# A hybrid attention layer on one core: first merge weights ahead of the attention outputs, and mixed blocks ahead of later gate weights on the load queue

## The chip, the cores and the metric

The kernel runs on one core of a Trainium2 chip. The metric is the device time of one execution in microseconds (us), as the median of several runs. A profile of one execution gives for each engine what ran when: PE is the matrix engine (PEld its weight loads), DVE the vector engine, ACT the scalar engine, POOL the third elementwise engine, and SP the engine that issues most of the loads and stores. Each engine works through its own list of instructions strictly in the listed order; an instruction whose data are not there holds up all that stand behind it on that engine.

## What is computed

One layer of an encoder, for 1024 tokens of width 1024, all in float32:

```python
proj = (rms_norm(x, g_norm1) * (1 + sc1) + sh1) @ w_in
qa, ka, va, qb, kb, vb, gates = split(proj)
o_a = neighbourhood_attention(qa, ka, va, rpb)            # 8 heads, 512 columns
o_b = dilated_window_attention_merged(qb, kb, vb)         # 3 groups of 4 heads, 256 columns after merging
gate_a, gate_b = split(sigmoid(gates + b_gate))
merged = gate_a * (o_a @ w_proj_a) + gate_b * (o_b @ w_proj_b)
x = x + gt1 * (merged @ w_o)
a, up = split((rms_norm(x, g_norm2) * (1 + sc2) + sh2) @ w_ffn_in)
x = x + gt2 * ((silu(a) * up) @ w_ffn_out)
```

The change lies in the part that computes `gates` (a product of the normalised input with 2048 columns of `w_in`) and then `merged`.

## The kernel before

Every float32 matrix operand is written as a sum of two parts of a narrower format that the matrix engine takes, called hi and lo. ACT copies the operand into hi (lines 124 and 1180), then DVE or POOL subtracts hi from the operand and writes lo (lines 125 and 1181). A product of two such operands is three matrix multiplications: hi by hi, hi by lo, lo by hi. The order of the matrix instructions on PE is the order of the program text. On the other engines a scheduler inside the compiler sets the order, from the program order and its own estimate of times, except that an instruction given to `pin` (`tc.keep_in_program_order`) keeps its place relative to the others that are pinned. The order is fixed when the kernel is built.

The gates are computed for eight blocks of 128 channels, each with a Strassen-like scheme of seven half-size products called w11, w12, x1, x4 and then x2, x3, w22. Here `prod` means 12 matrix multiplications of 128x128 by 128x512, for half of the depth. The four first products of each block run either inside the attention stage or, for blocks 3 and 4, right after it (`cover`). Then the three last products run in three groups (`gate_group`): blocks (3, 4, 5), then (6, 7, 2), then (0, 1); in each group x2 of all its blocks, then x3, then w22. So after the attention PE has 8 products of `cover`, 9 + 9 + 6 of the groups, 32 in all.

The right-hand operands of x2, x3 and w22 are sums and differences of blocks of the normalised input, the mixed blocks. They lie ready in device memory (`t_d`), and `mixed_load` brings one (two loads of 1 MB) into a part of the tile `hT` when its former content is no longer needed: x2 after w11, x3 after w12, and w22 after x4.

The weights of the last products come by `gate_late_load` (per block one load of 512 KB and one of 256 KB into a tile named `gl`), and `gate_late` makes of them x2, x3 and w22: two subtractions on DVE (lines 1124 and 1125), then hi and lo of each. lo of x2 and x3 is DVE's, lo of w22 is POOL's. `gate_late` of a block of the next group stands behind one of the three phases of a group. The results are added on DVE into accumulators named `sg` (line 1136), partly on POOL (line 1138), and go through a sigmoid on ACT (line 1092). `gate_acc` loads the partial sums of a block from the store `sig_d` into `sg`.

`w1_combos` prepares sums of weights for a much later stage: a load of 1 MB, four sums on DVE (lines 1115 to 1118) and four stores. `o_split` loads the attention outputs (six pieces, `o_d`, 512 KB each in two halves) into buffers named `raw` and splits them into the tiles `oT`; pieces 0 to 3 belong to the first attention, 4 and 5 to the second. `merge` computes a block of `merged` in two halves of 512 tokens: for each half 12 matrix multiplications of `oT` 0 to 3 (bank t or v), then 6 of `oT` 4 and 5 (bank d or s). Its weights come by `merge_w` (`wpa` and `wpb`, also through `raw`), with lo by POOL. There are six `raw` buffers, and six tiles that the gate weights, `w1_combos` and `oT` share in turn.

Of the kernel before, what the change touches and what calls it, by code (L numbers as in the profile page):

```python
# [25 lines left out]
EARLY = tuple(i for k in range(6) for i in (k, k + HT))  # L26
AHEAD, OTURN = 6, {1: 6, 5: 7}
MORD = (3, 4, 5, 6, 7, 2, 0, 1)
GPAIRS, GGROUPS = ((5, 6), (7, 2), (0, 1), (3, 4)), ((3, 4, 5), (6, 7, 2), (0, 1))
# [18 lines left out]
def hybrid_layer(ctx: ExitStack, tc: tile.TileContext, x, colp, wada1, wada2, bada2, wqkv, wg, wpa, wpb,  # L48
                 wo, w1, w2, hgain, ropeg, rope, rbias, bmask, g2r, out):
    nc = tc.nc  # L50
# [18 lines left out]
    t_d = tc.dram_tile([2, 4, 128, 4, 512], F32, name="t_d")  # L69
# [42 lines left out]
    def fview(ap):  # L112
        return ap.bitcast(F32)

    def wload(src, n):
        raw = wp.tile([128, 512], F32, tag="raw", bufs=NRAW, name="raw")
        nc.sync.dma_start(raw[:, :n], src)
        return raw[:, :n]

    def wsplit(r, eng=None):  # L120
        n = r.shape[1]
        hi = wp.tile([128, 512], F32R, tag="hi", bufs=NHL, name="whi")
        lo = wp.tile([128, 512], F32R, tag="lo", bufs=NHL, name="wlo")
        nc.scalar.activation(hi[:, :n], r, AF.Copy)  # L124
        (eng or nc.gpsimd).tensor_sub(lo[:, :n], r, fview(hi[:, :n]))  # L125
        return hi, lo

    def wslot(src, n):
        return wsplit(wload(src, n))
# [56 lines left out]
    def unit_load(u, k):  # L186
        return wload(wqkv[u, :, k, :], 384)
# [510 lines left out]
    def mm_set(pb, wsl, src, ksrc, n, ntot, done, hs):  # L698
        for j in range(n):
            for i, (a, b) in enumerate(PASS):  # L700
                nc.tensor.matmul(pb, wsl[a][:, j * 128:(j + 1) * 128], src[b][:, ksrc + j, hs],
                                 start=(done == 0 and j == 0 and i == 0),
                                 stop=(done + j == ntot - 1 and i == 2))

    gwt, gacc, gbank, graw = {}, {}, {}, {}

    def hblk(k, c):
        return [z[:, 4 * k:4 * k + 4, 512 * c:512 * c + 512] for z in hT]

    TBLK = {"w11": (0, 0), "w12": (1, 0), "x4": (1, 1), "x1": (0, 1), "x2": (0, 0), "x3": (1, 0), "w22": (1, 1)}  # L710
    TD = {"x1": 0, "w22": 1, "x3": 2, "x2": 3}

    def mixed_load(nm):
        for q in range(2):
            nc.sync.dma_start(fview(hblk(*TBLK[nm])[q]), t_d[q, TD[nm]])

    def gate_raw(i, q):
        return wload(wg[i, :, 4 * q:4 * q + 4, :], 512)

    def gate_land(z, i, q0, q1):  # L720
        nc.sync.dma_start(z[:, 512 * q0:512 * q1], wg[i, :, 4 * q0:4 * q1, :])
        for q in range(q0, q1):
            graw[i, q] = z[:, 512 * q:512 * q + 512]

# [5 lines left out]
    def gate_prep(p, part):  # L730
        pr = GPAIRS[p]
        if part == 0:
            for i in pr if p == 0 else ():
                for q in (0, 1):
                    graw[i, q] = gate_raw(i, q)
            for nm, q in (("w11", 0), ("w12", 1)):
                for i in pr:
                    gwt[i, nm] = wsplit(graw[i, q])
            return
        for i in pr:  # L740
            for q in (2, 3) if p == 0 else ():
# [13 lines left out]
    def gate_open_out(i, nm, p):  # L755
        c11, a, f, e = (gacc[i] + [None, None])[:4]
        if nm in ("w11", "x1"):
            nc.scalar.activation(a if nm == "w11" else f, p, AF.Copy)
        else:
            nc.vector.tensor_add(c11 if nm == "w12" else e, a if nm == "w12" else f, p)  # L760
# [29 lines left out]

    tpc = {}

    pin = tc.keep_in_program_order

    def t_piece(m, part):

# [168 lines left out]
    for n in range(6, 92):  # L965
# [87 lines left out]
        if n == 79:  # L1053
            mixed_load("x1")
# [21 lines left out]
    def sig_half():  # L1076
        return sgp.tile([128, 512], F32, tag="sg", bufs=26, name="sg")

    def gate_acc(i, load):
        a, f, e = gacc[i][1:] = [sig_half() for _ in range(3)]  # L1080
        if load:
            for m, z in ((1, a), (3, e), (2, f)):
                nc.sync.dma_start(z, sig_d[i, m])
        sig[i, 0, 1], sig[i, 1, 0], sig[i, 1, 1] = e, a, f
# [6 lines left out]
    def gate_sig(i, br, z):  # L1091
        nc.scalar.activation(z, z, AF.Sigmoid, bias=bg_c[:, 8 * br + i:8 * br + i + 1])
# [7 lines left out]
    def gate_prod(i, nm):  # L1100
        p = gate_bank()
        for k in range(4):
            gate_mm(p, gwt[i, nm], hblk(*TBLK[nm]), k)
        return p

    def gate_late_load(i):
        z = ttp.tile([128, 2048], F32, tag="t", bufs=6, name="gl")
        gate_land(z, i, 2, 4)
        gate_land(z, i, 0, 1)

    def w1_combos(n, j):
        z = ttp.tile([128, 2048], F32, tag="t", bufs=6, name="w1m")
        pin(nc.sync.dma_start(z, w1[j]))
        r = [z[:, 512 * q:512 * q + 512] for q in range(4)]
        pin(nc.vector.tensor_add(r[3], r[2], r[3]))
        nc.vector.tensor_sub(r[2], r[0], r[2])
        nc.vector.tensor_sub(r[0], r[3], r[0])
        nc.vector.tensor_sub(r[1], r[1], r[0])
        for q, y in enumerate((r[3], r[0], r[2], r[1])):
            nc.sync.dma_start(w1_d[n, q], y)  # L1120

    def gate_late(i):
        r = [graw.pop((i, q), None) for q in range(4)]
        nc.vector.tensor_sub(r[0], r[0], r[2])
        nc.vector.tensor_sub(r[2], r[3], r[0])
        gwt[i, "x2"] = wsplit(r[2], nc.vector)
        gwt[i, "x3"] = wsplit(r[0], nc.vector)
        gwt[i, "w22"] = wsplit(r[3])

    def gate_group(g, nxt):  # L1130
        for ph, nm in enumerate(("x2", "x3", "w22")):
            for i in g:
                p = gate_prod(i, nm)
                a, f, e = gacc[i][1:]
                z, br = ((e, 0), (f, 1), (a, 1))[ph]
                nc.vector.tensor_add(a, a, p)
                if ph < 2:
                    nc.gpsimd.tensor_add(z, z, a)
                gate_sig(i, br, z)
            for i in nxt[ph:ph + 1]:  # L1140
                gate_late(i)

    mw = {}
    mw = {}

    def merge_w(i):
        if i not in mw:
            mw[i] = wslot(wpa[i], 512), wslot(wpb[i], 256)

    def merge(i):  # L1150
        merge_w(i)
# [16 lines left out]
    def o_split(prs):  # L1168
        for pr in prs:
            oT[pr] = ttp.tile([128, 2, S], F32R, tag="t", bufs=6, name="oT")  # L1170
            for hf in range(2):
                hs = slice(hf * 512, hf * 512 + 512)
                raw = wp.tile([128, 512], F32, tag="raw", bufs=NRAW, name="raw")
                pin(nc.sync.dma_start(raw, o_d[pr][:, hs]))
                hi, lo = (oT[pr][:, b, hs] for b in range(2))
                if pr < 4:
                    hi, lo = (oT[pr][:, b].rearrange("p (r w) -> p w r", r=16)[:, 32 * hf:32 * hf + 32]
                              for b in range(2))
                    raw = raw.rearrange("p (w r) -> p w r", r=16)
                nc.scalar.activation(hi, raw, AF.Copy)  # L1180
                nc.vector.tensor_sub(lo, raw, fview(hi))
# [19 lines left out]
    def cover(nm):  # L1201
        for i in GPAIRS[3]:
            p = gate_prod(i, nm)
            gate_open_out(i, nm, p)
            if nm == "w12":
                gate_sig(i, 0, gacc[i][0])
# [3 lines left out]
        sig[i, 0, 0] = gacc[i][0]  # L1210
        gate_acc(i, False)
    gate_prep(3, 1)
    cover("w11")
    for i in GGROUPS[0][:2]:
        gate_late_load(i)
    mixed_load("x2")
    cover("w12")
    gate_late_load(5)
    mixed_load("x3")
    gate_acc(5, True)  # L1220
    gate_late(3)
    cover("x1")
    gate_late(4)
    for i in GGROUPS[1]:
        gate_late_load(i)
    cover("x4")
    mixed_load("w22")
    gate_late(5)
# [1 line left out]
    for n, g in enumerate(GGROUPS):  # L1230
        nxt = GGROUPS[n + 1] if n < 2 else ()
        for i in nxt:
            gate_acc(i, True)
        if n == 1:
            for i in nxt:
                gate_late_load(i)
            w1_combos(0, EARLY[0])
        gate_group(g, nxt)
        if n == 1:
            w1_combos(1, EARLY[1])  # L1240
        if n:
            o_split(((4, 5, 0), (1, 2, 3))[n - 1])
    h1l.release()
    h1p.release()
    h2p = pool("h2", "left")
# [2 lines left out]
    for n, i in enumerate(MORD):  # L1248
        for z in MORD[n:n + 2]:
            merge_w(z)  # L1250
        merge(i)
        for z in MC11.get(n, ()):
            c11_load(z)
        if n + 2 < 8:
            merge_w(MORD[n + 2])
        if n in MSLOT:
            wo_slot(MSLOT[n])
        if n in MKEEP:
            wo_keep(MKEEP[n])
# [454 lines left out]
```

## Time and profile before

| what | value |
|---|---|
| runs | 1512.48, 1511.18, 1508.93 us; median 1511.18 |
| the profiled execution | 1509.87 us, of which the span of the instructions is 1507.8 |
| granted PE clock, mean | 0.996 |
| busy: PE, DVE, ACT, POOL | 98%, 72%, 47%, 39% of the span |
| PE's waits between 600 and 790 us | 1.5 us before a w22 product, 7.4 and 1.0 us before the first merge |

A row of the timeline gives the start and the duration, the engine, the line, the operation, and `out<-in` by the program's names without their numbers; in brackets stands the idle time before it and what ended it. `x10` means ten instructions in one row, with their total. SPq is SP's queue: the row is the issue of a load or store, not its landing.

### The profile page before, as it was taken

How to read it: one execution, taken by the hardware profiler on the slowest of the kernel's cores; microseconds unless marked ns; L12 is line 12 of the kernel's file. 1: busy time of each engine (PE TensorE's matmuls, PEld its weight loads, DVE VectorE, ACT ScalarE, POOL GpSimd, SP SyncE). 2: the span in 40 equal slices, each digit the busy share in tenths (PEclk: the TensorE clock that was granted, in tenths of full speed). 3: DMA queues.
4: the chain of work that ended last, by engine and by line, in shares of the span. 5: the costliest groups of instructions: out<-in, count | busy, mean ns of one | idle time of the engine just before them, and what ended most of it. 6: DMA issues, size and time to landing. Idle time of an engine off the chain costs nothing.

```text
span 1507.8 us, 24306 instructions
## 1 busy us (share of the span) xinstructions
PE 1475.7 (98%) x8168; PEld 1259.8 (84%) x8168; DVE 1081.7 (72%) x2218; ACT 703.3 (47%) x1775; POOL 581.7 (39%) x572
## 2 busy tenths in 40 slices
PE   9999999999999999997999999999999999999998
PEld 7988989998888877876888888888888888887886
DVE  6867777766678755565774597788767777599468
ACT  5656666655766756345432344233223323354442
POOL 0432333211101123254432301677767776104464
PEclk9999999999999999998999999999999999999999
DMA  9626444645235453865452225345433334898353
GB/s 368 240 70 202 137 152 154 193 139 168 88 106 177 153 190 136 299 268 176 153 199 91 95 92 181 120 134 180 156 124 107 111 105 146 273 374 281 98 150 102
DMA packets 155756, 252.11 MB, mean 167 GB/s; under 512 B 26704, under 2 KB 70384, under 8 KB 154608
## 3 DMA queue, kind: packets, MB, share of 16 engines
q1 hardware_dynamic: 137056, 236.92, 47.3%
q10 hardware_dynamic: 18576, 13.64, 2.8%
q8 instruction: 65, 1.06, 0.3%
q14 instruction: 59, 0.48, 0.1%
HBM read 187.21 MB, written 63.29 MB: 166 GB/s over the span
## 4 chain that ended last, share of the span: by engine, by line
PE 81%; DVE 7%; DMA 7%; issue 2%; ACT 1%; POOL 1%; SPq 0%; DVEq 0%; ACTq 0%; POOLq 0%
PE ps_d L321 14%; PE ps_v L1379 7%; PE ps_d L1379 7%; PE ps_s L1379 7%; PE ps_t L1379 6%; PE ps_d L752 5%; PE ps_s L1549 3%; PE ps_d L1549 3%; PE ps_s L1314 2%; PE ps_d L1314 2%; PE ps_t L1549 2%; PE ps_v L1549 2%; DVE wlo L125 2%; PE ps_t L1159 2%; PE ps_v L1314 1%
## 5 line engine op out<-in xcount | busy, mean ns | idle before, releaser
L321 PE MATMUL ps_d<-whi,hT 128*128 128x384 f32 x1152 | 309.8, 340 | 0.0
L124 ACT ACTIVATE whi<-raw 128x512 fp32r<-128x512 f32 (+2 forms) x314 | 182.0, 595 | 199.3 <-PE ps_s L1549 42.3
L125 POOL TENSOR_TENSOR wlo<-raw,whi 128x512 fp32r<-128x512 f32 (+2 forms) x123 | 160.4, 1316 | 290.4 <-ACT whi L124 289.8
L125 DVE TENSOR_TENSOR wlo<-raw,whi 128x512 fp32r<-128x512 f32 (+1 forms) x191 | 168.7, 898 | 62.3 <-ACT whi L124 58.2
L321 PEld LDWEIGHTS ps_d<-whi,hT 128*128 128x128 f32 x1152 | 209.2, 188 | 1.2 <-issue 0.8
L321 PE MATMUL ps_d<-wlo,hT 128*128 128x384 f32 x576 | 193.0, 335 | 2.3 <-DVE wlo L125 2.2
L321 PEld LDWEIGHTS ps_d<-wlo,hT 128*128 128x128 f32 x576 | 108.4, 188 | 3.3 <-DVE wlo L125 2.8
L124 ACT ACTIVATE whi<-ws 128x512 fp32r<-128x512 f32 x60 | 37.7, 628 | 121.6 <-DVE ws L1396 77.5
L1329 POOL TENSOR_TENSOR e<-e,c 128x512 f32<-128x512 f32 x44 | 68.9, 1566 | 60.0 <-DVE c L1459 35.8
L752 PE MATMUL ps_d<-hT,whi 128*128 128x512 f32 x256 | 80.3, 395 | 0.0
L351 POOL TENSOR_TENSOR ra<-qn,rtab 128x64 f32<-128x64 f32 x48 | 16.7, 347 | 152.6 <-DVE qn L344 111.5
L125 POOL TENSOR_TENSOR wlo<-m,whi 128x512 fp32r<-128x512 f32 x35 | 51.4, 1479 | 55.0 <-ACT whi L124 55.0
L1327 ACT ACTIVATE e<-e 128x512 f32<-128x512 f32 x44 | 27.4, 630 | 88.4 <-DVE e L1462 60.7
L125 POOL TENSOR_TENSOR wlo<-gl,whi 128x512 fp32r<-128x512 f32 x26 | 34.6, 1341 | 82.4 <-ACT whi L124 79.5
L564 ACT ACTIVATE P<-P,st 128x256 f32<-128x256 f32 (+2 forms) x100 | 45.7, 459 | 35.0 <-DVE st L562 34.9
L1379 PE MATMUL ps_v<-h2T,whi 128*128 128x512 f32 x192 | 59.2, 389 | 0.0
L1379 PE MATMUL ps_s<-h2T,whi 128*128 128x512 f32 x192 | 59.1, 389 | 0.0
L1379 PE MATMUL ps_d<-h2T,whi 128*128 128x512 f32 x184 | 56.8, 390 | 0.0
L135 ACT ACTIVATE ry<-ss,eps 128x4 f32<-128x4 f32 (+1 forms) x88 | 26.2, 298 | 64.1 <-DVE ss L342 50.6
L1328 DVE TENSOR_TENSOR e<-e 128x512 f32<-128x512 f32 x44 | 42.5, 974 | 17.6 <-ACT e L1327 17.5
L752 PEld LDWEIGHTS ps_d<-hT,whi 128*128 128x128 f32 x256 | 47.1, 188 | 9.5 <-ACT PT L517 0.2
L310 DVE SCALAR_TENSOR_TENSOR acc<-wa,cact,acc 128x512 f32<-128x512 f32 x56 | 42.5, 758 | 17.2 <-DMA wa<-in_wada_dram 17.0
(412 smaller groups left out, 4049.4 us busy)
## 6 DMA issues: line engine op xcount, KB each, us to landing
raw<-in_w_dram SPq DMA_DIRECT2D x139, 256.0 KB, 3.8
ga_d<-e SPq DMA_DIRECT2D x77, 256.0 KB, 2.4
raw<-ga_d SPq DMA_DIRECT2D x77, 256.0 KB, 2.9
wa<-in_wada_dram SPq DMA_DIRECT2D x32, 512.0 KB, 5.2
raw<-in_wqkv_dram SPq DMA_DIRECT2D x80, 192.0 KB, 3.2
m<-in_w_dram SPq DMA_DIRECT2D x44, 256.0 KB, 5.8
xt<-in_x_dram SPq DMA_DIRECT2D x16, 512.0 KB, 9.5
land<-in_wada_dram SPq DMA_DIRECT2D x16, 512.0 KB, 10.0
```

The lines of the kernel that those rows point to most:

```text
L124: nc.scalar.activation(hi[:, :n], r, AF.Copy)
L125: (eng or nc.gpsimd).tensor_sub(lo[:, :n], r, fview(hi[:, :n]))
L310: nc.vector.scalar_tensor_tensor(ada_acc[c], wa, cact[:, kk:kk + 1], ada_acc[c], op0=ALU.mult, op1=ALU.add)
L321: nc.tensor.matmul(pd[:, :384], tok(a, k, t), U.w[k][b][:, :384], start=(k == 0 and i == 0), stop=(k == KT - 1 and i == 2))
L564: nc.scalar.activation(C.P[h][:nq, c], C.P[h][:nq, c], AF.Exp, scale=-1.0, bias=nm, accum_out=sm)
L752: nc.tensor.matmul(pb, w[x][:, k * 128:(k + 1) * 128], b[y][:, k], start=(k == 0 and q == 0), stop=(k == 3 and q == 2))
L1159: nc.tensor.matmul(pb, w[a][:, j * 128:(j + 1) * 128], oT[pr][:, b, hs], start=(j == 0 and q == 0), stop=(j == len(prs) - 1 and q == 2))
L1314: nc.tensor.matmul(pbs[hf], h2T[a][:, k, t * 128:(t + 1) * 128], wow[hf, k][b], start=(n == 0 and (a, b) == PASS[0]), stop=(n == KT - 1 an ...
L1328: nc.vector.tensor_mul(sg, sg, a)
L1329: nc.gpsimd.tensor_mul(sg, sg, up)
L1379: nc.tensor.matmul(pb, w[p][:, k * 128:(k + 1) * 128], b[q][:, k], start=(k == 0 and i == 0), stop=(k == 3 and i == 2))
L1549: nc.tensor.matmul(pb[m], o[0][a][:, m * 128:(m + 1) * 128], o[1][b], start=(k == 0 and i == 0), stop=(k == HT - 1 and i == 2))
```

## The change

In front of the merge of the first two blocks (3 and 4) their weights are now loaded and split ahead of the attention outputs: `merge_w` is called for them before the last gate group, and its loads are pinned. `o_split` moves from behind the groups into the last group, two pieces after each of its three phases, in the order 0 to 5 (it was 4, 5, 0 after the second group and 1, 2, 3 after the third). The loads of mixed blocks and of late gate weights are pinned in program order, and that order changes: the loads of blocks 3 and 4 stand before the first `cover`, and the loads for blocks 6, 7, 2, 0 and 1 behind the mixed block w22, each behind its partial sums. Both `w1_combos` stand together before the second group.

```diff
-    def wload(src, n):
+    def wload(src, n, keep=False):
         raw = wp.tile([128, 512], F32, tag="raw", bufs=NRAW, name="raw")
-        nc.sync.dma_start(raw[:, :n], src)
+        d = nc.sync.dma_start(raw[:, :n], src)
+        if keep:
+            tc.keep_in_program_order(d)
         return raw[:, :n]
...
     def mixed_load(nm):
         for q in range(2):
-            nc.sync.dma_start(fview(hblk(*TBLK[nm])[q]), t_d[q, TD[nm]])
+            pin(nc.sync.dma_start(fview(hblk(*TBLK[nm])[q]), t_d[q, TD[nm]]))
...
     def gate_land(z, i, q0, q1):
-        nc.sync.dma_start(z[:, 512 * q0:512 * q1], wg[i, :, 4 * q0:4 * q1, :])
+        pin(nc.sync.dma_start(z[:, 512 * q0:512 * q1], wg[i, :, 4 * q0:4 * q1, :]))
...
             for i in nxt[ph:ph + 1]:
                 gate_late(i)
+            if not nxt:
+                o_split((2 * ph, 2 * ph + 1))
...
-    def merge_w(i):
+    def merge_w(i, keep=False):
         if i not in mw:
-            mw[i] = wslot(wpa[i], 512), wslot(wpb[i], 256)
+            mw[i] = [wsplit(wload(w[i], n, keep)) for w, n in ((wpa, 512), (wpb, 256))]
...
-    cover("w11")
     for i in GGROUPS[0][:2]:
         gate_late_load(i)
+    cover("w11")
     mixed_load("x2")
+    gate_late_load(5)
     cover("w12")
-    gate_late_load(5)
     mixed_load("x3")
     gate_acc(5, True)
     gate_late(3)
     cover("x1")
     gate_late(4)
-    for i in GGROUPS[1]:
-        gate_late_load(i)
     cover("x4")
     mixed_load("w22")
     gate_late(5)
...
         for i in nxt:
             gate_acc(i, True)
+            gate_late_load(i)
         if n == 1:
-            for i in nxt:
-                gate_late_load(i)
-            w1_combos(0, EARLY[0])
+            for j in range(2):
+                w1_combos(j, EARLY[j])
+        if n == 2:
+            for i in MORD[:2]:
+                merge_w(i, True)
         gate_group(g, nxt)
-        if n == 1:
-            w1_combos(1, EARLY[1])
-        if n:
-            o_split(((4, 5, 0), (1, 2, 3))[n - 1])
```

Line numbers grow by three at most in the changed kernel. PE's list is the same in both kernels, instruction for instruction. Three places where the lists of the other engines differ:

SP's list before, from the first load of gate weights that follows the mixed block x3's partial sums: four loads of gate weights (`gl`, blocks 0 and 1) stand ahead of the mixed block w22 (`hT`), and all partial sums (`sg`) behind it.

```order
L1083 DMA sg<-sig_d 128x512 x3
L721 DMA gl<-in_wg_dram 128x1024
L721 DMA gl<-in_wg_dram 128x512
L721 DMA gl<-in_wg_dram 128x1024
L721 DMA gl<-in_wg_dram 128x512
L715 DMA hT_408<-t_d 128x4x512
L715 DMA hT_114<-t_d 128x4x512
```

SP's list now, at the same place: the two parts of w22 are directly behind the partial sums of block 5, and the gate weights of blocks 6, 7 and 2 come behind them, each after its block's partial sums.

```order
L718 DMA hT_408<-t_d 128x4x512
L1085 DMA sg<-sig_d 128x512 x3
L724 DMA gl<-in_wg_dram 128x1024
L724 DMA gl<-in_wg_dram 128x512
L1085 DMA sg<-sig_d 128x512 x3
L724 DMA gl<-in_wg_dram 128x1024
L724 DMA gl<-in_wg_dram 128x512
```

The gate weights of blocks 7 and 2 move behind w22 on the queue with this, from ahead of the mixed block x3.

DVE's list before, where the weights of block 7 (`gl_8955`) and block 2 (`gl_8958`) are split. `ps_v_9023` is the product x2 of block 3, `ps_d_9039` and `ps_s_9055` x2 of blocks 4 and 5, `ps_t_9085`, `ps_v_9101` and `ps_d_9117` x3 of blocks 3, 4 and 5. `gl_9218` and `gl_9221` belong to blocks 0 and 1. The splits `wlo_9136` (x2 of block 7) and `wlo_9195` (x2 of block 2) stand among these, eight and five products ahead of their use on PE:

```order
L1136 TENSOR_TENSOR sg_8794<-sg_8794,ps_d_9039 128x512
L125 TENSOR_TENSOR wlo_9136<-gl_8955,whi_9135 128x512
L1136 TENSOR_TENSOR sg_8890<-sg_8890,ps_s_9055 128x512
L1136 TENSOR_TENSOR sg_8790<-sg_8790,ps_t_9085 128x512
L125 TENSOR_TENSOR wlo_9140<-gl_8955,whi_9139 128x512
L1124 TENSOR_TENSOR gl_9218<-gl_9218 128x512
L1125 TENSOR_TENSOR gl_9218<-gl_9218 128x512
L1136 TENSOR_TENSOR sg_8794<-sg_8794,ps_v_9101 128x512
L1124 TENSOR_TENSOR gl_9221<-gl_9221 128x512
L1125 TENSOR_TENSOR gl_9221<-gl_9221 128x512
L1136 TENSOR_TENSOR sg_8890<-sg_8890,ps_d_9117 128x512
L125 TENSOR_TENSOR wlo_9195<-gl_8958,whi_9194 128x512
```

DVE's list now, at the start of the second group. `ps_d_9244` is the product x2 of block 6 and `ps_s_9260` that of block 7; `gl_9011` and `gl_9020` are the weights of blocks 7 and 2:

```order
L1138 TENSOR_TENSOR sg_8996<-sg_8996,ps_d_9244 128x512
L127 TENSOR_TENSOR wlo_9136<-gl_9011,whi_9135 128x512
L127 TENSOR_TENSOR wlo_9140<-gl_9011,whi_9139 128x512
L1126 TENSOR_TENSOR gl_9020<-gl_9020 128x512
L1127 TENSOR_TENSOR gl_9020<-gl_9020 128x512
L1138 TENSOR_TENSOR sg_9005<-sg_9005,ps_s_9260 128x512
L127 TENSOR_TENSOR wlo_9195<-gl_9020,whi_9194 128x512
```

The split for x2 of block 7 now stands behind the result of x2 of block 6, and that for block 2 behind the result of block 7: behind the product that comes just ahead of its use on PE.

SP's list before, around the attention outputs: the twelve loads of `o_d` follow the last stores of the prepared sums, and the merge weights follow them.

```order
L1113 DMA w1m<-in_w_dram 128x2048
L1120 DMA w_d<-w1m 128x512 x4
L1174 DMA raw<-o_d 128x512 x12
L117 DMA raw<-in_wpa_dram 128x512
L117 DMA raw<-in_wpb_dram 128x256
```

SP's list now, at the same place:

```order
L1115 DMA w1m<-in_w_dram 128x2048
L1122 DMA w_d<-w1m 128x512 x4
L117 DMA raw<-in_wpa_dram 128x512
L117 DMA raw<-in_wpb_dram 128x256
L117 DMA raw<-in_wpa_dram 128x512
L117 DMA raw<-in_wpb_dram 128x256
L1178 DMA raw<-o_d 128x512 x12
```

The four merge weights take four of the six `raw` buffers ahead of the attention outputs. ACT's list goes the same way: the hi parts of these four weights now stand before the first hi part of `oT`, and before they stood behind the last.

More of the change, by code (lines that the diff above doesn't have):

```diff
@@ L703, in mm_set @@
                                  stop=(done + j == ntot - 1 and i == 2))
+    pin = tc.keep_in_program_order
     gwt, gacc, gbank, graw = {}, {}, {}, {}
@@ L791, in hybrid_layer @@
     tpc = {}
-    pin = tc.keep_in_program_order
     def t_piece(m, part):
```

## The prediction

> **What bounds the kernel now.** I read the page first, then PE's waits from 600 to 790 us, then that stretch in the timelines of all engines.
>
> ```profile
> span 1507.8 us, 24306 instructions
> PE 1475.7 (98%) x8168; PEld 1259.8 (84%) x8168; DVE 1081.7 (72%) x2218; ACT 703.3 (47%) x1775; POOL 581.7 (39%) x572
> PE ps_t L1159 <- ACT whi L124: 7.4, 1, 7.4
> PE ps_s L752 <- DMA hT<-t_d: 1.5, 1, 1.5
> PE ps_t L1159 <- POOL wlo L125: 1.0, 1, 1.0
> ```
>
> PE is busy for 98%, and its list of instructions is the same after the change. So only PE's waits and its clock can move. The three waits named are all that PE has in this stretch: one before a w22 product (bank s, L752), two at the first merge (L1159).
>
> ```profile
> 650.48 0.73 PE L752 MATMUL ps_s<-hT,whi 128*128 128x512 f32 x2 [1.53 <-DMA hT<-t_d]
> 699.35 0.39 PE L752 MATMUL ps_t<-hT,wlo 128*128 128x512 f32 x1
> 707.12 1.22 PE L1159 MATMUL ps_t<-oT,whi 128*128 128x512 f32 x2 [7.38 <-ACT whi L124]
> ...
> 650.48 3.02 PE ps_s L752 x12
> 653.50 2.72 PE ps_t L752 x12
> 709.29 4.63 PE ps_t L1159 x10
> 715.88 2.72 PE ps_v L1159 x12
> 718.60 1.36 PE ps_s L1159 x6
> ...
> 650.00:655.00 5.00, 4.52 (x20) 3.75 (x21) 3.61 (x5) 1.58 (x3) 2.88 (x2) 1.00 1.05 401
> 703.00:705.00 2.00, 0.00 (x0) 0.00 (x0) 1.21 (x2) 2.00 (x4) 0.00 (x0) 0.96 0.37 59
> 714.00:715.00 1.00, 1.00 (x3) 0.72 (x3) 0.65 (x1) 0.90 (x2) 1.00 (x2) 0.50 0.85 194
> 715.00:716.00 1.00, 1.00 (x6) 0.83 (x5) 0.08 (x1) 0.00 (x0) 1.00 (x3) 0.97 0.57 200
> ```
>
> The last three columns of a stretch are PE's granted clock, the DMA share and GB/s. A product takes 2.72 us. The last gate product ends at E = 699.74 (699.35 + 0.39); the first half merge (12 + 6 multiplications, 2.72 + 1.36 = 4.08 at full clock, as in the second half) ends at 715.88. So it loses 715.88 - 699.74 - 4.08 = 12.1 us: 8.3 of waiting, the rest at half clock. The clock fell about 5 us into the long wait and came back at 715; after the 1.53 us wait it stayed at 1.00.
>
> **Part 1, the mixed block w22.**
>
> ```profile
> 632.71 4.61 SPq L721 DMA_DIRECT2D gl<-in_wg_dram  x4
> 639.64 1.20 SPq L715 DMA_DIRECT2D hT<-t_d  x2
> ```
>
> w22 overwrites the block that x4 reads, and x4 ends when x2 begins, about 632.5 (six products before 648.95, the start of the wait). SP issued it only at 639.64, behind the loads for blocks 0 and 1, and it landed by 650.4. Now it goes at 632.5, with x3 and 0.75 MB ahead of it; 2 MB at the 401 GB/s above take 5 us, so it lands by about 642, 7 us early. This frees 1.53 us, and 0.3 us of the slower first product (3.02 against 2.72): **-1.8 us**. Ends: 0 if the load were late again, -1.8.
>
> **Part 2, gate weights of blocks 7 and 2.** Their loads have some 8 us to spare at that rate, but their splits now stand on DVE behind the result of the product just ahead of their use.
>
> ```profile
> 659.04 0.69 DVE L1136 TENSOR_TENSOR sg<-sg,ps_v 128x512 f32<-128x512 f32 x1 [2.03 <-PE ps_v L752]
> 659.65 0.68 DVE L125 TENSOR_TENSOR wlo<-gl,whi 128x512 fp32r<-128x512 f32 x1
> 662.90 1.78 DVE L1115 TENSOR_TENSOR w1m<-w1m 128x512 f32<-128x512 f32 x1
> 662.46 1.67 POOL L1138 TENSOR_TENSOR sg<-sg 128x512 f32<-128x512 f32 x1 [4.38 <-DVE sg L1136]
> ```
>
> The result takes DVE 0.1 + 0.6 us after PE's product, the split 0.7; PE needs lo at its third multiplication, 0.45 us after the product. That is 1.0 us of PE wait for block 7 and 1.0 for block 2, at least. For block 2 DVE must also do block 7's second split and two subtractions before that, and ACT the hi part after them. POOL adds into `sg` right then, and an operation of DVE between two SBUF tensors that meets POOL took 1.78 instead of 0.68. I take one such meeting for block 2: 1.05 + 2.05 = **+3.1 us**. Ends: +2.0 (no meeting) and +5.4 (one for block 7, three for block 2, 1.1 each). I take the value with one, since DVE operations that follow without a gap keep their 0.68.
>
> The Trainium skill, "Advanced Engine Details and Errata", section "GPSIMD Details", says that the Pool engine shares a read and a write interface with DVE and conflicts with DVE instructions that have two SBUF inputs. The trace agrees (1.78 against 0.68). Taken for every operation here, the rule speaks against the change: part 2 would cost its upper end, and the sum below would be 2.3 us higher.
>
> **Part 3, the first merge.** SP's rows before, and the splits:
>
> ```profile
> 669.48 0.38 SPq L1113 DMA_DIRECT2D w1m<-in_w_dram  x1
> 687.86 11.95 SPq L1174 DMA_DIRECT2D raw<-o_d  x12
> 700.51 0.33 SPq L117 DMA_DIRECT2D raw<-in_wpa_dram  x1
> 703.26 1.92 ACT L1180 ACTIVATE oT<-raw 128x512 fp32r<-128x512 f32 x2
> 706.45 0.93 ACT L124 ACTIVATE whi<-raw 128x512 fp32r<-128x512 f32 x2
> 707.14 10.99 POOL L125 TENSOR_TENSOR wlo<-raw,whi 128x512 fp32r<-128x512 f32 x10 [4.54 <-ACT whi L124]
> L1180 ACT ACTIVATE oT<-raw x12: 616/1059/1164, 691.8 to 705.6; 128x512 fp32r<-128x512 f32 x12
> L1181 DVE TENSOR_TENSOR oT<-raw,oT x12: 679/1105/1782, 692.5 to 707.0; 128x512 fp32r<-128x512 f32 x12
> L1092 ACT ACTIVATE sg<-sg,cp x26: 675/725/727, 622.4 to 707.3; 128x512 f32<-128x512 f32 x26
> raw<-o_d SPq DMA_DIRECT2D x12, 256.0 KB, 3.0
> gl<-in_wg_dram SPq DMA_DIRECT2D x6, 1024.0 KB, 6.6
> ```
>
> Before, merge weights were issued behind all twelve loads of `o_d` and split behind all twelve splits (hi at 706.45, lo from 707.14): that is the wait. Now they are ahead, and PE waits for the attention outputs. Going back from the new E:
>
> - SP's second `w1m` load follows the first one's sums, which stand on DVE behind x3 of block 2 (E-24.5): issued at E-21. A load of 1 MB took 6.6 us in the median; I take 6, to E-15. Its sums wait on DVE, the last three behind w22 of block 2 (E-16.3): done at E-12, stored at E-11.7.
> - Four weight loads and two of `o_d` at 0.33 each: `o_d` from E-10, landed (3.0) at E-7.
> - The weights hold four of the six `raw` buffers. The next two loads of `o_d` wait for POOL's split of the first weights (landed E-8, hi 0.63, lo 1.3): issued E-6, landed E-3. The others follow the splits of `oT`.
> - ACT then has, up to the half that the first half merge needs last (piece 5): six splits at 1.06, three at 0.62, three sigmoids at 0.7, and about 1 us for a load: 11.3, so E+8.3. DVE's lo comes 1 us later, PE's last multiplications 0.5 later: E+9.8 to E+9.9, against E+4.08.
>
> So **5.8 us** of waiting, in pieces of at most 1.3 us, as 1.06 and 1.1 us splits arrive one by one; at such pieces I keep the clock at 1.00. Ends: 1.5 (only the last splits late) and 12.1 (as before); I take the middle value because every step has a row. The weights of the next merges are 16 us away and cost nothing: POOL's ten splits took 10.99.
>
> **Part 4, loads of gate weights inside the attention stage** are issued later, because the stores of partial sums now go ahead:
>
> ```profile
> 532.04 0.33 SPq L721 DMA_DIRECT2D gl<-in_wg_dram  x1
> 538.74 14.45 SPq L787 DMA_DIRECT2D sig_d<-gc  x5
> 554.10 0.60 ACT L783 ACTIVATE ga<-ps_d 128x512 f32<-128x512 f32 x1
> ```
>
> The first moves from 532.0 to about 539; it lands 6.6 us later, is split by 547, and its product runs at 551 (result at 554.10). The slack of about 4 us covers it: 0. If it were short by 1 us, that would be +1.
>
> **The sum.** 1509.87 is the profiled execution (span 1507.8 and 2.07 around it). -1.8 + 3.1 - 12.1 + 5.8 = -5.0, so 1504.9; the median of the runs, 1511.18, lies 1.31 above that execution, so 1506.2 for a median.
>
> **The rivals.**
>
> *All hidden.* If `o_d` lands sooner than my chain has it, only the last splits are late (1.5), and part 2 costs 2.0: -1.8 + 2.0 - 12.1 + 1.5 = -10.4, 1500.8. For it: SP issues in 0.33 us and loads land in 3.0. Against it: the six buffers and the order on ACT.
>
> *No gain.* A wait at the first merge lasts until the clock falls: the half clock costs 12.1 - 8.3 = 3.8 again, so 9.6 at the merge, and part 2 is at its upper end, 5.4: +1.1, 1512.3. Against it: the pieces are short. The Trainium skill, "TensorE: Matmul & The Clock Gate", section "What's actually happening", says that the clock halves after at least one idle window of about 3.4 us, free-running. The fall 5 us into the wait and the 1.00 after 1.53 us agree. By it my pieces would leave the sum as it is.
>
> *Slower: the second `w1m` load.* DVE stops at its first sum until it lands, with gate results behind. Should it land 11 us after its issue instead of 6, `o_d` moves by 5 us, the first wait for `oT` exceeds 5 us and the half clock returns: 5.8 + 5 + 3.8 = 14.6 at the merge, sum +3.8, 1515.0. It decides from a landing about 10 us after the issue. For it: SP's queue is in order and 1 MB of stores goes ahead. Against it: the median of 6.6.
>
> *The order does not matter*, because w22 or the merge waits for something else that is as late: within 3 us of before.
>
> **Chances and range.** Forecast (gain 3 to 8 us) 0.52, all hidden 0.20, no gain with the last rival 0.18, slower 0.10. 0.2% is 3 us, about what a measurement can tell here: faster 0.72, same 0.18, slower 0.10. The range takes in the all-hidden case and the no-gain case: 1500 to 1512.5.
>
> **What would show it.** The w22 wait is gone, hT issued near 632.5. Two new PE waits on `wlo` at the second and third product of the second group, 1 and 2 us. The first merge waits in pieces on `oT` splits and no longer on `whi` L124, with the clock at 1.00. The forecast fails if a single wait at the merge exceeds 5 us, if SP's loads of `o_d` start later than E-8, or if PE waits inside the attention stage.

## The result and the profile after

The changed kernel is slower: 1515.46 us in the median of 19 runs (1512.22 to 1523.27) against 1508.65 us before (19 runs), a ratio of 1.0057 with a 95% interval of 1.0043 to 1.0071. The forecast was 1506.2 us. The profiled execution took 1517.23 us, 7.4 more than the one before.

The head of the page of the changed kernel (its line numbers are 2 to 4 higher than before):

```profile
span 1515.4 us, 24287 instructions
PE 1483.9 (98%) x8168; PEld 1263.8 (83%) x8168; DVE 1088.1 (72%) x2218; ACT 703.2 (46%) x1775; POOL 580.2 (38%) x572
```

PE's waits between 600 and 760 us:

```profile
PE ps_t L1163 <- DVE oT L1185: 5.9, 4, 2.2
PE ps_v L755 <- DMA hT<-t_d: 3.7, 2, 2.1
PE ps_t L755 <- ACT whi L126: 2.4, 1, 2.4
PE ps_t L1163 <- ACT oT L1184: 1.1, 1, 1.1
PE ps_t L755 <- DVE wlo L127: 1.0, 1, 1.0
PE ps_s L755 <- DVE wlo L127: 0.4, 1, 0.4
PE ps_s L755 <- ACT whi L126: 0.3, 1, 0.3
```

The wait for hi of the merge weights is gone, as forecast, and so is the wait at w22. In their place stand waits at the first merge, at the splits of the gate weights, and one that the forecast had put at nothing: 3.7 us for the mixed block x2 (`ps_v`, L755), at the start of the first gate group. The same in PE's timeline:

```profile
632.07 0.77 PE L755 MATMUL ps_v<-hT,whi 128*128 128x512 f32 x1 [2.10 <-DMA hT<-t_d]
634.46 0.80 PE L755 MATMUL ps_v<-hT,whi 128*128 128x512 f32 x1 [1.63 <-DMA hT<-t_d]
664.01 0.73 PE L755 MATMUL ps_s<-hT,whi 128*128 128x512 f32 x2 [0.26 <-ACT whi L126]
665.14 0.50 PE L755 MATMUL ps_s<-hT,wlo 128*128 128x512 f32 x1 [0.39 <-DVE wlo L127]
670.05 0.73 PE L755 MATMUL ps_t<-hT,whi 128*128 128x512 f32 x2 [2.36 <-ACT whi L126]
671.76 0.50 PE L755 MATMUL ps_t<-hT,wlo 128*128 128x512 f32 x1 [0.98 <-DVE wlo L127]
706.58 0.39 PE L755 MATMUL ps_t<-hT,wlo 128*128 128x512 f32 x1
708.03 0.50 PE L1163 MATMUL ps_t<-oT,whi 128*128 128x512 f32 x1 [1.06 <-ACT oT L1184]
710.40 0.70 PE L1163 MATMUL ps_t<-oT,whi 128*128 128x512 f32 x1 [1.87 <-DVE oT L1185]
714.13 0.79 PE L1163 MATMUL ps_t<-oT,whi 128*128 128x512 f32 x1 [2.17 <-DVE oT L1185]
```

And two stretches of all engines, with PE's clock in the third column from the right:

```profile
632.00:638.00 6.00, 4.31 (x9) 3.10 (x10) 4.88 (x6) 1.32 (x4) 1.26 (x1) 0.50 1.05 410
711.00:724.00 13.00, 8.96 (x20) 5.59 (x19) 12.90 (x15) 10.13 (x15) 4.84 (x4) 0.50 0.77 222
```

Two lengths are compared in all that follows. The *gate stretch* runs from the first product of the cover (610.71 before, 608.04 now) to the end E of the last gate product. Its 32 products need 32 x 2.72 = 87.0 us. It took 89.0 us before (E = 699.74) and 98.9 now (E = 706.58 + 0.39 = 706.97). The *first half merge* ended at E+16.0 before (its successor in bank v starts at 715.72) and ends at E+15.9 now (722.87). So the gate stretch lost 9.9 us, and the first merge, where 6.3 us were to be won, gave 0.1. Of the 11.9 us above 87.0, some 6.5 lie at the product x2 of block 3 (PE was free at 629.97, the product ended at 639.12) and some 5 at the splits of blocks 7 and 2. The rest of the difference between the two executions: the attention stage ended 2.7 us earlier in this one, and the half clock cost 0.7 us in the second half merge; 9.9 - 0.1 - 2.7 + 0.7 = 7.8, of 7.4 measured. The 2.7 us need not come from the change: the kernel before and e12 (below), whose programs are the same up to there, differ by 3.7 us at the same point (610.71 and 607.04).

Where the mixed block x2 got late is seen in the timelines of SP and DVE. Before:

```profile
577.93 0.87 SPq L721 DMA_DIRECT2D gl<-in_wg_dram  x2
605.10 0.69 DVE L125 TENSOR_TENSOR wlo<-gl,whi 128x512 fp32r<-128x512 f32 x1 [1.35 <-ACT whi L124]
616.11 1.37 SPq L715 DMA_DIRECT2D hT<-t_d  x2
```

Now, with POOL, and in the last row from SP's waits:

```profile
596.24 0.87 SPq L724 DMA_DIRECT2D gl<-in_wg_dram  x2
607.95 5.04 POOL L127 TENSOR_TENSOR wlo<-gl,whi 128x512 fp32r<-128x512 f32 x4 [4.21 <-ACT whi L126]
619.26 0.69 DVE L127 TENSOR_TENSOR wlo<-gl,whi 128x512 fp32r<-128x512 f32 x1 [0.76 <-ACT whi L126]
620.03 1.76 SPq L724 DMA_DIRECT2D gl<-in_wg_dram  x4
621.83 1.29 SPq L718 DMA_DIRECT2D hT<-t_d  x2
SPq L724 <- DVE wlo L127: 10.2, 1, 10.2
```

The first row of each is the third and last pair of gate weights inside the attention stage. It is issued 18.3 us later (596.24 against 577.93), behind stores of partial sums. So its last split ends at 619.95 instead of 605.79. SP waits 10.2 us for that split (1.7 us before), since the next loads (blocks 3 and 4) take the memory that it frees. The mixed block x2 stands behind those loads on the queue in both kernels, and goes at 621.83 instead of 616.11. PE needs it at 629.97.

### The profile page after: what moved, and what is told of

It reads as the page before. It is cut to its first block, busy times and chain, and to the rows that moved or that the text cites. A ratio compares the mean times of both kernels' runs of the same rounds, so it can differ in the third digit from the quotient of the medians.

```text
span 1515.4 us, 24287 instructions
## 1 busy us (share of the span) xinstructions
PE 1483.9 (98%) x8168; PEld 1263.8 (83%) x8168; DVE 1088.1 (72%) x2218; ACT 703.2 (46%) x1775; POOL 580.2 (38%) x572
## 5 line engine op out<-in xcount | busy, mean ns | idle before, releaser
L755 PE MATMUL ps_d<-hT,whi 128*128 128x512 f32 x256 | 80.3, 395 | 0.0
L755 PEld LDWEIGHTS ps_d<-hT,whi 128*128 128x128 f32 x256 | 47.1, 188 | 9.6 <-ACT PT L519 0.2
```

Source lines behind the costliest of these rows:

```text
L755: nc.tensor.matmul(pb, w[x][:, k * 128:(k + 1) * 128], b[y][:, k], start=(k == 0 and q == 0), stop=(k == 3 and q == 2))
```

## The experiments

All were timed in five rounds beside the kernel before. "Ratio" is to the kernel before.

**e1_att_unpinned: the loads inside the attention stage without the pin.**

```diff
-    def gate_land(z, i, q0, q1):
-        pin(nc.sync.dma_start(z[:, 512 * q0:512 * q1], wg[i, :, 4 * q0:4 * q1, :]))
+    def gate_land(z, i, q0, q1, keep=True):
+        d = nc.sync.dma_start(z[:, 512 * q0:512 * q1], wg[i, :, 4 * q0:4 * q1, :])
+        if keep:
+            pin(d)
...
-            gate_land(z[:, j], i, 0, 4)
+            gate_land(z[:, j], i, 0, 4, False)
```

> The changed kernel, but the three 2 MB loads of gate weights inside the attention stage are not pinned, which puts them back to their old places among the stores of partial sums; all else stays. Theory A (the pin makes the third of them 18 us late, its splits then hold up the next gate loads and the mixed blocks behind them on SP): PE's two waits for hT of 2.10 and 1.63 us in the cover products and the half clock after them go, the stretch from the first x1 product of the cover to the last gate product shrinks from 98.9 us to about 91 (before: 89.0), and the time falls by 6 to 8 us, to about 1508 to 1510. Theory B (the waits come from the new order of the loads behind the attention, since two more loads stand ahead of the mixed blocks x2 and x3): the waits stay within 1 us of 3.7 and the time within 2 us of the changed kernel's 1515.

Measured: 1507.21 us, ratio 0.9998 (0.9979 to 1.0016), 8.2 us below the changed kernel. The gate stretch is 87.2 us without one wait: theory A, and better than its 91. The third pair of loads is issued at 576.89 and the mixed block x2 at 614.97, close to their places before. Not only the two waits for hT are gone but also the four at the splits of blocks 7 and 2. The run unpins all three pairs; that the third is the one that counts is read from the rows above. The rest of PE's waits stands at the first merge, which still ends at E+15.9 (E = 696.54):

```profile
696.96 0.51 PE L1165 MATMUL ps_t<-oT,whi 128*128 128x512 f32 x1 [0.42 <-ACT oT L1186]
699.18 0.50 PE L1165 MATMUL ps_t<-oT,whi 128*128 128x512 f32 x1 [1.72 <-DVE oT L1187]
701.82 0.79 PE L1165 MATMUL ps_t<-oT,whi 128*128 128x512 f32 x1 [1.67 <-DVE oT L1187]
703.90 0.80 PE L1165 MATMUL ps_t<-oT,whi 128*128 128x512 f32 x1 [0.87 <-ACT oT L1186]
705.57 0.80 PE L1165 MATMUL ps_t<-oT,whi 128*128 128x512 f32 x1 [0.86 <-DVE oT L1187]
707.65 0.80 PE L1165 MATMUL ps_t<-oT,whi 128*128 128x512 f32 x1 [0.43 <-DVE oT L1187]
```

Six waits make 6.0 us. Two stretches around them:

```profile
696.00:700.00 4.00, 1.86 (x7) 0.78 (x5) 3.97 (x4) 2.66 (x4) 1.36 (x2) 1.00 0.24 73
701.00:713.00 12.00, 8.93 (x16) 4.51 (x17) 11.03 (x13) 9.51 (x15) 6.84 (x3) 0.50 0.71 215
```

The clock is at 1.00 until 700 us, though PE is busy for 1.86 of 4 us, and at one half for the 12 us from 701.

**e3_merge_alone and e4_loads_alone: the two halves of the change apart.** e3 is the kernel before with `merge_w` ahead (with `wload` and `merge_w` as in the change), `o_split` in the last group and both `w1_combos` together; e4 is e1 with those three undone.

```diff
 # e3, against the kernel before
+            if not nxt:
+                o_split((2 * ph, 2 * ph + 1))
...
-            w1_combos(0, EARLY[0])
+            for j in range(2):
+                w1_combos(j, EARLY[j])
+        if n == 2:
+            for i in MORD[:2]:
+                merge_w(i, True)
         gate_group(g, nxt)
-        if n == 1:
-            w1_combos(1, EARLY[1])
-        if n:
-            o_split(((4, 5, 0), (1, 2, 3))[n - 1])
```

> The kernel before with only the merge part of the change: merge weights of blocks 3 and 4 pinned ahead of the attention outputs, o_split in the last group, both w1_combos together; no load of gate weights or mixed blocks is pinned or moved. Theory A (the chain of the second w1m load, its sums and stores still holds o_d until about 6 us before the last gate product, and many short waits halve the clock as one long wait does): from the last gate product to the end of the first half merge 14 to 17 us (before 16.1, changed kernel 15.9), the time within 3 us of before. Theory B (the prediction's chain holds when the gate part does not disturb it): 9.9 us, clock 1.00, the time 5 to 7 us below before.

> The kernel before with only the load part of the change, the loads inside the attention stage unpinned as in the run before last: w22 right behind x4, the gate weights of blocks 6, 7, 2, 0, 1 behind it; merge as before. Theory A (the wait for w22 goes, the splits of blocks 7 and 2 cost about 4.0 us of PE waits as in the changed kernel's trace): the stretch from the first x1 product of the cover to the last gate product about 91 us against 89.0, the time 2 to 4 us above before. Theory B (prediction's figures: -1.8 + 3.1): +1.3 us. Theory C (the loads behind w22 are so late that the first merge moves with the w1m loads behind them): over 5 us above before, with the excess at the merge.

Measured: e3 1501.67 us, ratio 0.9951 (0.9931 to 0.9970); e4 1510.08 us, ratio 1.0008 (0.9990 to 1.0026). e4 has a gate stretch of 87.2 us, again 1.8 below before and with no wait at the splits, so its theory A was wrong on the 4 us; its first merge waits 8.6 us for hi, 1.2 more than before. Alone, the merge part does what was forecast and more: in e3 the first half merge ends at E+4.5, with one wait of 0.3 us. So the two halves of the change work against each other: together, in e1, they are 5.5 us above e3. The rows of e3 on DVE, SP and PE:

```profile
664.61 1.78 DVE L1117 TENSOR_TENSOR w1m<-w1m 128x512 f32<-128x512 f32 x1
684.01 14.02 SPq L1178 DMA_DIRECT2D raw<-o_d  x12
701.79 0.70 PE L1163 MATMUL ps_t<-oT,whi 128*128 128x512 f32 x2 [0.34 <-DVE sg L1138]
```

Those of e1 on DVE and SP:

```profile
672.25 1.78 DVE L1119 TENSOR_TENSOR w1m<-w1m 128x512 f32<-128x512 f32 x1
689.86 16.00 SPq L1180 DMA_DIRECT2D raw<-o_d  x12
```

In e3 (E = 701.45) the first sum of `w1_combos` is at E-36.8 and the loads of `o_d` start at E-17.4; in e1 (E = 696.54) at E-24.3 and E-6.7. In e1 the gate weights of five blocks have moved behind w22, and their subtractions and splits stand ahead of these sums on DVE.

e3 gave back part of its 11.4 us: PE waited 1.9 us between two merges and 2.6 us at the output projection, followed by 3 us at half clock (timeline, then a stretch):

```profile
772.81 1.81 PE L1318 MATMUL ps_d<-wr,h2T 128*128 128x512 f32 x4 [2.61 <-DVE sg L1167]
773.00:776.00 3.00, 3.00 (x8) 2.38 (x8) 2.31 (x4) 1.67 (x3) 1.26 (x2) 0.52 0.66 216
```

The bank is not free, because DVE has not yet multiplied the last merge's result (L1167).

**e5_one_w1m, e6_w1m_ahead, e7_one_block, e9_no_pool_add: what makes the first merge late in e1.** Each is e1 with one edit:

```diff
 # e5: and EARLY[:2] -> EARLY[:1] in the three places that use the prepared sums
-            for j in range(2):
+            for j in range(1):
                 w1_combos(j, EARLY[j])
 # e6
-        if n == 1:
-            for j in range(2):
-                w1_combos(j, EARLY[j])
+        if n < 2:
+            w1_combos(n, EARLY[n])
 # e7
-            for i in MORD[:2]:
+            for i in MORD[:1]:
                 merge_w(i, True)
 # e9
-                    nc.gpsimd.tensor_add(z, z, a)
+                    (nc.gpsimd if nxt else nc.vector).tensor_add(z, z, a)
```

> The first of these runs (loads in attention unpinned), with only one w1_combos ahead of the second group instead of two; the sums of the other block of weights are made later where they are used, on DVE and POOL, as for all further blocks. Theory A (the second w1m load, which waits for the first one's sums on DVE and whose own sums and stores stand ahead of o_d on SP, sets when o_d is loaded): o_d is issued 10 us or more ahead of the last gate product, the first half merge ends 5 to 10 us behind it instead of 16, at a clock of 1.00, and the time is 6 to 10 us below the first of these runs. Theory B (the six raw buffers and ACT's order set it): o_d is issued earlier, but the loads wait for buffers, the waits for oT stay above 5 us, and the time is within 2 us of the first of these runs.

> The kernel of e1 (loads in attention unpinned), with the first w1_combos moved ahead of the first of the three gate groups, so that its load and sums stand ahead of the gate weights of blocks 0 and 1; the second stays ahead of the second group. Theory A (in e1 the splits of the gate weights that moved behind w22 push the w1m sums back on DVE, and these push o_d back on SP to 6.7 us ahead of the last gate product E; merged alone, e3, it was 17.4 us): o_d is issued 10 us or more ahead of E, the first half merge ends at E+4.5 to E+9, the gate stretch stays at 87.2 us, and the time is 7 to 11 us below e1 (1507.2), less up to 4 us for a new wait at the output projection: 1499 to 1504. Theory B (ACT and POOL set it, not the loads): first half merge at E+13 or later, time within 3 us of e1.

> The kernel of e1, with the merge weights of only one block (3) ahead of the attention outputs instead of two; those of block 4 follow the attention outputs. Two of the six raw buffers are held instead of four. Theory A (the late start of o_d sets the end, the buffers little): the first half merge ends 2 to 3 us earlier than the E+15.9 of e1, because two loads, two hi and two lo parts go out of the way, time 1 to 3 us below e1. Theory B (the four buffers held until POOL's splits set the rate of the o_d loads, as the prediction had it): over 5 us earlier.

> The kernel of e1 with the additions into sg of the last gate group on DVE instead of POOL. In e1 one of these took 4.19 us on POOL beside DVE's splits, ACT's sigmoid waited 2.13 us for it, and ACT's next splits of oT stood behind that sigmoid. Theory A (POOL's starved additions hold ACT up in the middle of the splits): the first half merge ends 2 to 5 us earlier than E+15.9, time 2 to 4 us below e1. Theory B (ACT's wait is off the chain): within 1.5 us of E+15.9 and of e1's time.

| kernel | o_d loads from | first half merge ends | wait at the output projection | time, us | ratio (95%) |
|---|---|---|---|---|---|
| e1 | E-6.7 | E+15.9 | 0 | 1507.21 | 0.9998 (0.9979 to 1.0016) |
| e5 | E-15.6 | E+9.2 | 2.2 | 1503.07 | 0.9961 (0.9947 to 0.9974) |
| e6 | E-9.6 | E+10.3 | 1.1 | 1506.22 | 0.9989 (0.9976 to 1.0003) |
| e7 | E-7.8 | E+11.3 | 4.6 | 1507.92 | 1.0003 (0.9988 to 1.0017) |
| e9 | E-6.9 | E+12.7 | 1.3 | 1507.46 | 0.9995 (0.9980 to 1.0011) |
| e3 | E-17.4 | E+4.5 | 2.6 | 1501.67 | 0.9951 (0.9931 to 0.9970) |

Every suspect is a part of it: the second `w1m` load (6.7 us), the place of the sums (5.6), the four buffers with their splits (4.6), POOL's additions (3.2). They overlap, as their sum exceeds the 11.4 between E+15.9 and the E+4.5 of e3. In e5 and e6 PE no longer waits for the attention outputs at the start of the merge but 3.4 and 3.7 us for the bank, whose gate result DVE had not yet fetched; the clock then fell in e5 too (0.50 from 700 to 702 us), against its theory A. For e7 the 4.6 us lie between its two theories; e6 ended 1.3 us behind the latest end in its theory A. The time hardly follows: e5 is 4.1 us below e1 and not 6 to 10, and e6, e7 and e9 are within 1 us of e1. Part of what they win at the first merge turns up at the output projection (in e6 also 1.9 us between two merges).

**e8_filled_wait: is it the half clock?**

```diff
         gate_group(g, nxt)
+    pfill = bank("v")
+    for _ in range(2):
+        for k in range(4):
+            gate_mm(pfill, gwt[GGROUPS[2][-1], "w22"], hblk(*TBLK["w22"]), k)
     h1l.release()
```

> The kernel of e1 with 24 more matrix multiplications on PE (two products, 5.4 us, of operands that lie ready; their result is not read) between the last gate product and the first merge. Nothing else changes on the other engines in this stretch. Theory A (the last split of the attention outputs, 14.8 us behind E in e1, sets the end, and the half clock in between only shows that PE idles): the clock stays at 1.00 for longer, the first half merge still ends 14.8 to 16.5 us behind E, and the time is within 2 us of e1. Theory B (the half clock costs the 5.8 us by which the loss of 11.8 us exceeds the waits of 6.0): the clock stays at 1.00, the first half merge ends near E+10, and the time falls by about 5 us.

Measured: 1512.78 us, ratio 1.0031 (1.0018 to 1.0045). At the first merge theory A holds (stretches, and PE's wait behind them). The clock stayed at 1.00 to 710 us, 12.4 us behind the last real gate product (697.62), and the first half merge still ended 15.2 us behind it, against 15.9:

```profile
703.00:706.00 3.00, 1.65 (x8) 1.03 (x6) 3.00 (x4) 3.00 (x4) 0.84 (x1) 1.00 0.58 186
706.00:710.00 4.00, 1.67 (x6) 0.97 (x6) 4.00 (x5) 2.63 (x6) 1.25 (x1) 1.00 0.55 158
710.00:713.00 3.00, 2.78 (x8) 1.95 (x7) 3.00 (x5) 2.77 (x5) 1.29 (x2) 0.54 0.66 213
PE ps_d L1321 <- DVE sg L1169: 2.6, 1, 2.6
```

So most of what the first half merge lost is not the half clock: with it put off, the end moved by 0.7 us. The last five multiplications, from 710.48, ran at half clock again; at 2.72 us for twelve they would have taken 1.1 instead of 2.3, so 1.2 us more is the most that can be put down to it. PE's waits before that, 1.70 and 1.99 us, are for DVE's splits, and DVE was busy in all 10 us of these three stretches: it sets the end. The whole kernel was 5.6 us slower than e1, not within 2. A wait of 2.6 us came up at the output projection (last row), and the waits for splits in the last product of the layer grew from 1.2 to 3.5 us; why is open.

**e10 to e13: is DVE the bound behind the first merge?** e10 is e3, e12 the kernel before and e13 e5, each with the first edit; e11 is e3 with the second.

```diff
-            nc.vector.tensor_sub(h2T[1][:, i, hs], m, fview(h2T[0][:, i, hs]))
+            nc.gpsimd.tensor_sub(h2T[1][:, i, hs], m, fview(h2T[0][:, i, hs]))
 # e11
-            wow[hf, k] = wsplit(wo_raw(hf, k), nc.vector if hf else None)
+            wow[hf, k] = wsplit(wo_raw(hf, k))
```

> The kernel of e3 (merge part alone) with the lo parts of the merged result (h2T) subtracted on POOL instead of DVE. In e3 the first merge ended 11.4 us earlier relative to the last gate product, but the time fell by 7 us only: PE waited 1.88 us in the merges and 2.61 us, with some 1.2 us of half clock, for DVE at the output projection. Theory A (DVE cannot follow the merges once they start early: some 4.2 us per half against PE's 4.08, 0.7 us of it waiting for ACT before the lo part): the wait of 2.6 us at the output projection is gone or under 1 us, and the time falls by 2 to 4 us below e3's 1501.7. Theory B (POOL, at 1.3 us per subtraction beside the weights' lo parts, now falls behind and slows DVE's operations in SBUF): the merges wait for weights, and the time is at e3's or above.

> The kernel of e3 with three lo parts of output weights in the merge stage on POOL instead of DVE (3 operations of 0.87 us). Theory A (DVE's total work sets the wait of 2.61 us at the output projection): the wait shrinks to 0 to 1 us, time 1.5 to 3 us below e3. Theory B (these three stand in gaps in which DVE waits for ACT, and each POOL operation that they become lengthens one of DVE's): the wait stays above 2 us, time within 1 us of e3.

> The kernel before with the h2T lo parts on POOL, nothing else. Control for the run with the same edit on the merge part: before, PE waits nowhere between the first merge and the down projection, so DVE has time. Theory A: no change, within 1.5 us of before. Theory B (the edit gains by itself, whatever the first merge does): 2 to 4 us below before.

> The kernel of e5 (changed kernel, loads in attention unpinned, one w1_combos) with the h2T lo parts on POOL. e5 has no w22 wait, a first half merge at E+9.2, and a wait of 2.20 us at the output projection. Theory A: that wait goes, 2 to 3 us below e5's 1503.1. Theory B: as for the first of these runs, no gain.

Measured: e10 1500.47 us, ratio 0.9943 (0.9920 to 0.9966); e11 1500.18 us, 0.9946 (0.9927 to 0.9964); e12 1508.09 us, 1.0001 (0.9987 to 1.0016); e13 1500.02 us, 0.9939 (0.9923 to 0.9956). The wait at the output projection is gone in e10, e11 and e13; these are all that PE's waits between 690 and 790 us hold in e10 and e13:

```profile
PE ps_t L1163 <- DVE sg L1138: 1.9, 1, 1.9
...
PE ps_t L1165 <- DVE sg L1140: 3.2, 1, 3.2
```

In the kernel before the same edit changes nothing (e12), which fits that there the long wait at the first merge gives DVE the time to follow. Against e3 the step in the ratio is far smaller than the intervals (0.0008 and 0.0005, or 1.2 and 1.5 us, of 2 to 4 and 1.5 to 3 expected); against e5 it is 0.0022, or 3.1 us, with intervals that overlap. So what is shown is that the wait vanished, and not a gain in time. e13, e11 and e10 beat the kernel before by 8 to 9 us and the changed one by some 15; they can't be told apart.

## Why the prediction was wrong

The sum had the gate stretch at +1.3 us (-1.8 + 3.1) and the first merge at -6.3 (5.8 - 12.1). In the profiled execution they came to +9.9 and -0.1. Two terms failed: part 4, put at 0, and the 5.8 us of part 3. Without the first error (e1) the kernel is level with the one before; the second alone takes the gain away.

- **Part 1 was right.** The wait for w22 is gone in the changed kernel, in e1 and in e4; the gate stretch of e1 and e4 is 1.83 us shorter than before (forecast -1.8).
- **Part 4 is the first step that failed.** It was priced at 0 with an upper end of 1, from the first of three pairs of loads alone. That pair was issued 3.0 us later (535.08 against 532.04; forecast 7), in an execution whose attention stage ended 2.7 us earlier, and PE waited for none of the three inside the attention stage. The third pair moved by 18.3 us and is the one that loads behind the attention stage wait for. Price: 3.73 us of waits for x2, and the clock at one half from 632.0 to 638.8. With the splits below, undoing the pin gave 98.9 - 87.2 = 11.7 us in the gate stretch and 8.2 in the medians (e1). The forecast had named "PE waits inside the attention stage" as the sign of this; it came right behind it.
- **Part 2 was of the right size for the order as built, 4.0 us against 3.1** (0.65 + 3.34, forecast 1.05 + 2.05), but its cause lay in part 4: in e1, e4 and e5, with the pin away, DVE's list has them early enough, and there is no wait at all. In e1 the splits for block 2 (659.90) stand ahead of the result of block 6 (661.11); in the changed kernel even those for block 7 (664.40) stand behind it (663.79). The reason for counting one meeting with POOL does not hold: the subtraction of 1.78 us in the prediction's own rows (662.90) follows without a gap on a split from 662.30, and in the changed kernel the two splits from 664.40 take 2.37 us, the subtraction from 666.70 takes 1.77, and the two splits from 670.03 take 3.37.
- **Part 3 is the second step that failed: the sum of the waits came out, the end of the merge did not.** Forecast: 5.8 us in pieces, clock 1.00, end at E+9.9. In e1 it is 6.0 us in six pieces and half the clock, end at E+15.9, so the agreement of 5.8 and 6.0 is luck. In the changed kernel the end is E+15.9 as well, and the loads of `o_d` start at E-5.5, later than the E-8 that the prediction named as a sign of failing:

```profile
701.50 15.44 SPq L1178 DMA_DIRECT2D raw<-o_d  x12
```

  The chain of which every link had a row was late in two links, as e1 shows. The loads of `o_d` start at E-6.7, not E-10, because the first sums of `w1m`, which begin at E-24.3 as forecast, take DVE 6.4 us instead of 3.5 (672.25 to 678.64: one meets POOL and takes 1.78, another 1.67, and results and a split stand between). Then ACT's splits, due in 11.3 us, take 15.7 (694.88 to 710.5), of which ACT waits 4.7, the second and third row of its waits in e1 between 690 and 713 us:

```profile
ACT whi L126 <- DMA raw<-in_wpa_dram: 3.3, 2, 2.2
ACT oT L1186 <- DMA raw<-o_d: 2.6, 2, 2.2
ACT sg L1096 <- POOL sg L1142: 2.1, 1, 2.1
ACT whi L126 <- DMA raw<-in_wpb_dram: 0.2, 1, 0.2
```

  The addition on POOL that the third row waits for:

```profile
704.55 4.19 POOL L1142 TENSOR_TENSOR sg<-sg 128x512 f32<-128x512 f32 x1 [1.64 <-DVE sg L1140]
```

  It took 4.19 us beside DVE's splits, and ACT's sigmoid waits for it, with splits of `oT` behind. The trace before has its like (4.16 us), and the sum of ACT's work left it out:

```profile
698.45 4.16 POOL L1138 TENSOR_TENSOR sg<-sg 128x512 f32<-128x512 f32 x1 [2.91 <-DVE sg L1136]
```

  The Trainium skill, "Advanced Engine Details and Errata", section "GPSIMD Details", says that the Pool engine shares an interface with DVE. The trace agrees, but from the other side than the prediction took it: here POOL is the one held up. DVE's three splits beside this addition take 3.20 us, and in e9, with no addition on POOL, two take 2.11: the same 1.1 each. e9 won 3.2 us at the merge by taking the additions off POOL.
- **"At such pieces I keep the clock at 1.00" was wrong.** The clock fell just after 700 us in e1, after 4 us with PE busy for 1.86 and no wait above 1.72. The Trainium skill, "TensorE: Matmul & The Clock Gate", section "What's actually happening", has the clock fall after an idle window of about 3.4 us; in e1 it fell after a piece of that length (696.83 to 700.24) in which PE was busy for 43%, so short waits count together. Yet e8 shows that at most 2 us of the merge's loss hang on it.
- **The rivals.** "Slower" named 1515.0 us, and 1515.46 was measured, but that is luck: the second `w1m` load landed 5 us after its issue (690.60, first sum at 695.81), not 11. "No gain" had the half clock at the merge (9.6 us lost; 11.8 measured) but not the waits for x2. "All hidden" came true for the merge in e3 alone. That the two parts of the change disturb each other through DVE's list was none of the rivals.

## What to carry to other kernels

A pin that moves a series of loads is priced by the last of them and by what waits for the memory that it frees, not by the first. Before a wait on the engine that is 98% busy is counted as won, ask which other engine used that wait to catch up: here it was DVE, and in e7 all of the 4.6 us won at the first merge turned up again at the output projection. Where DVE was relieved (e10, e11, e13) that wait was gone. Two moves that each shorten their own stretch alone (e4 the gates, e3 the merge) may use the same slack, so they are costed together in the list of the engine that they share.

## What was not expected of the hardware

PE's clock halved in e1 when PE was busy for 47% of 4 us (1.86 of 4.00) with no wait above 1.72 us, and stayed at one half for 12 us while PE was busy for 74% (8.93 of 12.00). It stayed at 1.00 over 7 us with PE busy for 47% in e8 (3.32 of 7.00, 703 to 710).

The two fit together when the time is cut where the clock itself changes. In e1 it was at one half from 700.24 to 713.89 us, which is four times 3.41. In the 3.41 us ahead of the fall PE was busy for 1.47 (43%), and in the last 3.41 ahead of the rise for 3.37. In e8 the clock fell at 710.26; in the 3.41 us ahead of that PE was busy for 1.42 (42%), and in the 3.41 before those, after which the clock stayed, for 1.71 (50%). So in these two runs a piece of 3.41 us decides, with a border between 43% and 50%. The border isn't sharp: in the changed kernel the clock stayed after a piece with 45% (1.54, 666.15 to 669.56), and in e9 it fell after one with 49% (1.67, 702.20 to 705.62).
